# Two attention layers on one core: whole differential rows on VectorE, all key-tile remainders on GpSimd

## The chip, the core and the metric

The kernel runs on one core of one Trainium2 chip. The metric is the device time of one execution in microseconds; less is better. Five engines work at the same time, each through its own queue in order: TensorE (PE: matrix products and transposes; PEld is its weight load), VectorE (DVE), ScalarE (ACT), GpSimd (POOL), and SyncE (SP), which issues the DMAs. An instruction that waits holds up everything behind it on its engine.

## The reference

Two layers, each with one input projection that feeds three parallel branches (a state space scan, grouped-query attention, differential attention) and one output projection. 256 context tokens stand ahead of 1024 latent tokens; latent tokens read all 1280 keys, context tokens the 256 context keys. The part that matters here is the differential branch: 4 heads, two softmax maps each over the same values.

```python
def diff_attend(q, k, v, p):
    o = attention(q[:, :, 0::2], k[:, :, 0::2], v) - lam * attention(q[:, :, 1::2], k[:, :, 1::2], v)
    o = (rmsnorm(o, norm_g) * (1.0 - lam_init)).astype(v.dtype)
    return o.reshape(o.shape[0], o.shape[1], DIFF_WIDTH) * jax.nn.silu(p["dg"])
```

All is float32.

## The kernel before, in words

The program runs, for each layer, the projections with the scan (from 0 to about 571 us, and from about 1070 to 1572 us) and then the attention of both kinds, with the output projection woven into it (571 to 1070 us, and 1572 to 1995 us), and a short end. The change lies in the attention.

Attention is cut into jobs: one kind (0 grouped-query, 1 differential), one head, two or four tiles of 128 queries. A job has two sides.

The score side (`s_pair`, `s_rows`): for a tile of 128 queries PE makes the scores of 1280 keys in three PSUM banks (tile `sc`, L1259), DVE takes each from PSUM, negated and with the least value kept (L1261, into the row tile `pt`), and ACT makes the exponential of the whole row of 1280 with its sum (L1274). A differential tile of queries has two such rows. They are combined before they meet the values: row 0 plus a factor times row 1, the factor (`cc`, L1304 and L1305) being one number for each query. The combination is one DVE instruction over the columns from 0 to `cut` (L1308); what lies behind `cut` is done by two POOL instructions (L1312 scales a part of row 1, L1313 adds it to row 0). `cut` is the number of key tiles, 10, times `DC[l]`, rounded up, times 128:

```python
cut = math.ceil(jb.nk * DC[l]) * P                                   # L1307
V.scalar_tensor_tensor(dst[0][:, 0:cut], dst[1][:, 0:cut], c[:, 1:2], dst[0][:, 0:cut], ...)   # L1308
if cut < w_:
    a, b = dst[0][:, cut:w_], dst[1][:, cut:w_]
    G.tensor_scalar(b, b, c[:, 1:2], 1.0, op0=ALU.mult, op1=ALU.mult)  # L1312
    G.tensor_tensor(a, a, b, op=ALU.add)                               # L1313
```

A context job has two key tiles, so that its whole row lies within `cut` before and after.

The value side (`w_front`, `w_back`): in each step PE transposes two key tiles of two query tiles into one PSUM bank (`tp`, L1388). The product with the values runs in two fast float32 passes, so each 512 columns are split into a high part `ph` and a remainder `pl`. There are two ways. In the first, ACT rounds `tp` to `ph` (L1394) and DVE takes the remainder from PSUM (`pl<-tp,ph`, L128, the line of the helper `lo_part`). In the second, ACT copies `tp` to SBUF (`pf`, L1398), ACT or DVE in turn rounds it to `ph` (L1408 or L1410), and POOL takes the remainder (`pl<-pf,ph`, L128). `MIX` is the share of steps that go the first way while there are scores left to make; once the last scores of a layer are made, `MIXE` (0.5) holds instead. In a tenth of the last steps of layer 1 (`MIXF`) there is no split. PE then multiplies `ph` (L1430) and `pl` (L1431) with the values, three steps behind the transposes (`LAG`); `ph`, `pl` and `pf` share 8 buffers (`PWB`).

The order on each engine comes from a scheduler that goes through the whole program with its own timing of the instructions, so that another instruction in one place can move others on every engine. The tile pools add the waits.

Of the kernel before, what the change touches and what calls it, by code (L numbers as in the profile page):

```python
# [34 lines left out]
NPM = PK["convw"][0]  # L35
TOUT = 1
LEAD = 30
MIX = ((0.1, 0.1), (0.1, 0.1))
MIXE = 0.5
MIXC = ((0.5, 0.5), (0.4, 0.6))  # L40
DC = (0.8, 0.8)
MIXF = ((0.0, 0.0), (0.0, 0.1))
PWB = 8
CORD = ((0, 0), (1, 0), (1, 1), (0, 1), (1, 2), (1, 3), (0, 2), (0, 3))
# [23 lines left out]
def block_kernel(ctx: ExitStack, tc: tile.TileContext, tok, cvec, wmod, pack,  # L68
# [61 lines left out]
    def cs(c):  # L130
        return slice(c * P, (c + 1) * P)
# [303 lines left out]
    for l in range(DEPTH):  # L435
# [810 lines left out]
        with pool("att", 2) as ap, pool("attX", NXO, space=PSUM) as aX, pool("attO", NPO, space=PSUM) as aO, \  # L1246
# [49 lines left out]
            def s_pair(jb, pair):  # L1296
# [4 lines left out]
                if jb.kind == 1:  # L1301
# [4 lines left out]
                    w_ = jb.nk * P  # L1306
                    cut = math.ceil(jb.nk * DC[l]) * P  # L1307
                    V.scalar_tensor_tensor(dst[0][:, 0:cut], dst[1][:, 0:cut], c[:, 1:2], dst[0][:, 0:cut],  # L1308
# [74 lines left out]
            def w_front(jb, hf, s):  # L1383
# [3 lines left out]
                for j in range(4):  # L1387
                    TE.transpose(tp[:, j * P:(j + 1) * P], jb.pt[2 * hf + j % 2][:, cs(2 * s + j // 2)], ident)  # L1388
                mix[0] += MIX[l][jb.ph] if sdone[0] < len(squeue) else MIXE
                if mix[0] >= 1.0:  # L1390
# [250 lines left out]
```

## Time and profile before

| | us |
|---|---|
| median of 3 runs (2024.3 to 2028.09) | 2027.06 |
| the profiled execution | 2032.17 |
| its span, first to last instruction | 2030.4 |
| PE busy in the span | 1793.4 |
| DVE busy | 1369.5 |
| POOL busy | 1192.1 |
| ACT busy | 1046.7 |
| attention of layer 0 (571 to 1070) | 499 |
| attention of layer 1 (1572 to 1995) | 423 |

Busy times are sums over the span; an engine that is busy for a smaller part of it can still be what another waits for at a given place, so the waits of PE within the two attention stretches are read apart. In the rows further down a group names line, engine, operation, written and read tile, shape and count, then busy time, mean duration in ns, the idle time of the engine just before, and what ended it. In a timeline a row has its start, its duration (both us), the engine and the instruction; in brackets the idle time before it and who ended that.

### The profile page before, as it was taken

To read this page: it belongs to the slowest core of one execution; us is meant where nothing else is said; L and a number is where in the kernel's file an instruction comes from. 1 tells how busy PE (TensorE), PEld (TensorE's weight loads), DVE (VectorE), ACT (ScalarE), POOL (GpSimd) and SP (SyncE) were. 2 spreads that over 40 slices of the span, in tenths; PEclk is the share of its full clock that TensorE was granted. 3 is DMA by queue.
4 is the path that set the end of the run, shared out by engine and by line. 5 is a ranking of instruction groups with operands and counts; after the bars stand their busy time and mean duration, and the time that the engine had idled before them with its cause. 6 is when DMAs were issued, how large, how long until landed. Compare 5 with 4: busy or idle time off the path is not lost. (4 is left out here: it accounts for less than half of the span.)

```text
span 2030.4 us, 30265 instructions
## 1 busy us (share of the span) xinstructions
PE 1793.4 (88%) x9936; PEld 1457.8 (72%) x9936; DVE 1369.5 (67%) x3268; ACT 1046.7 (52%) x1971; POOL 1192.1 (59%) x1129
## 2 busy tenths in 40 slices
PE   5899999799989999988888899887899898988886
PEld 4687777687768578867675687776777677867774
DVE  3676568754566776796937586587645787887944
ACT  3554233333457766776545354333234577777651
POOL 2536355656637667777645344566566467877661
PEclk8899999899989999989799999998989999999987
DMA  9148657865787887786646158668657956566536
GB/s 285 53 129 281 206 165 204 266 221 181 226 264 237 279 283 244 230 254 196 209 166 219 46 193 268 192 196 264 210 158 213 298 158 193 163 178 204 176 117 219
DMA packets 359997, 418.57 MB, mean 206 GB/s; under 512 B 38752, under 2 KB 252832, under 8 KB 359840
## 3 DMA queue, kind: packets, MB, share of 16 engines
q1 hardware_dynamic: 359840, 416.64, 66.1%
q8 instruction: 78, 1.28, 0.3%
q14 instruction: 79, 0.65, 0.1%
HBM read 282.18 MB, written 134.38 MB: 205 GB/s over the span
## 5 line engine op out<-in xcount | busy, mean ns | idle before, releaser
L128 POOL TENSOR_TENSOR pl<-pf,ph 128x512 fp32r<-128x512 f32 x283 | 375.3, 1330 | 193.4 <-DVE ph L1410 97.7
L1261 DVE TENSOR_SCALAR_CACHE_REDUCE pt<-sc 128x512 f32<-128x512 f32 (+1 forms) x600 | 335.1, 586 | 104.8 <-PE sc L1259 90.5
L1274 ACT ACTIVATE pt<-pt,nm 128x1280 f32<-128x1280 f32 x192 | 262.2, 1366 | 109.9 <-DVE nm L1272 109.1
L976 PE MATMUL prj<-wh,u 128*128 128x512 f32 (+1 forms) x768 | 289.2, 381 | 7.3 <-ACT wh L965 5.4
L977 PE MATMUL prj<-wl,u 128*128 128x512 f32 (+1 forms) x768 | 289.3, 378 | 3.5 <-DVE wl L128 1.8
L978 PE MATMUL prj<-wh,u 128*128 128x512 f32 (+1 forms) x768 | 286.7, 375 | 0.0
L1388 PE MATMUL tp<-ident,pt 128*128 128x128 f32 x1312 | 210.3, 283 | 13.0 <-ACT pt L1274 6.2
L1398 ACT COPY pf<-tp 128x512 f32<-128x512 f32 x289 | 166.7, 581 | 81.4 <-PE tp L1388 50.1
L1431 PE MATMUL po<-pl,vt 128*128 128x256 f32 x644 | 179.7, 302 | 21.9 <-POOL pl L128 21.4
L1430 PE MATMUL po<-ph,vt 128*128 128x256 f32 x644 | 185.0, 301 | 11.7 <-ACT ot L1435 5.6
L1388 PEld LDWEIGHTS tp<-ident,pt 128*128 128x128 f32 x1312 | 161.9, 146 | 34.4 <-ACT pt L1274 8.0
L976 PEld LDWEIGHTS prj<-wh,u 128*128 128x128 f32 x768 | 149.5, 195 | 31.5 <-ACT wh L965 6.6
L977 PEld LDWEIGHTS prj<-wl,u 128*128 128x128 f32 x768 | 150.1, 196 | 29.8 <-DVE wl L128 4.5
L978 PEld LDWEIGHTS prj<-wh,u 128*128 128x128 f32 x768 | 150.0, 195 | 21.4
L1259 PE MATMUL sc<-dk,q 128*128 128x512 f32 (+1 forms) x400 | 148.9, 414 | 17.8 <-DVE pt L1261 9.6
L1431 PEld LDWEIGHTS po<-pl,vt 128*128 128x128 f32 x644 | 124.7, 194 | 38.0 <-POOL pl L128 32.0
L1430 PEld LDWEIGHTS po<-ph,vt 128*128 128x128 f32 x644 | 124.8, 194 | 32.6 <-ACT ot L1435 9.3
L1259 PE MATMUL sc<-gk,q 128*128 128x256 f32 (+1 forms) x400 | 117.4, 401 | 20.7 <-DVE pt L1261 10.1
L612 DVE SCALAR_TENSOR_TENSOR cacc<-craw,hw,cacc 128x1284 f32<-128x1284 f32 (+1 forms) x64 | 119.2, 1863 | 24.2 <-ACT cacc L609 17.3
L348 PE MATMUL ops<-y,wo 128*128 128x512 f32 (+1 forms) x304 | 118.6, 390 | 10.6 <-DMA y<-y 7.1
L587 PE MATMUL prj<-u,wTh 128*128 128x512 f32 x256 | 105.7, 413 | 14.0 <-ACT craw L603 5.6
L349 PE MATMUL ops<-y,wo 128*128 128x512 f32 (+1 forms) x304 | 114.3, 376 | 0.0
(277 smaller groups left out, 4233.1 us busy)
## 6 DMA issues: line engine op xcount, KB each, us to landing
wo<-wo SPq DMA_DIRECT2D x80, 512.0 KB, 4.5
wm<-in_wmod_dram SPq DMA_DIRECT2D x48, 512.0 KB, 5.8
dk<-dk SPq DMA_DIRECT2D x16, 1280.0 KB, 8.1
ab<-acs SPq DMA_DIRECT2D x18, 1024.0 KB, 6.8
wf<-in_wtok_dram SPq DMA_DIRECT2D x64, 256.0 KB, 3.9
wo<-wos SPq DMA_DIRECT2D x32, 512.0 KB, 3.5
y<-y SPq DMA_DIRECT2D x30, 512.0 KB, 6.1
op<-o SPq DMA_DIRECT2D x48, 256.0 KB, 4.2
```

Of the source, the lines that this page charges most:

```text
L128: eng.tensor_tensor(out_, full, hi.bitcast(F32), op=ALU.subtract)
L612: V.scalar_tensor_tensor(acc[:, a0:1284], raw[:, a0 + j:1284 + j], hw[:, i * 5 + j:i * 5 + j + 1], acc[:, a0:1284], op0=ALU.mult, op1=ALU.add)
L976: TE.matmul(ps[:, c0:], uh, wh[k][:, c0:], start=k == 0, stop=False)
L977: TE.matmul(ps[:, c0:], uh, wl[k][:, c0:], start=False, stop=False)
L978: TE.matmul(ps[:, c0:], ul, wh[k][:, c0:], start=False, stop=k == KT - 1)
L1259: TE.matmul(ps[:, 0:b - a].rearrange("p (t c) -> p t c", c=P), q[:, jb.q0 + j], kt[:, a // P:b // P], start=x == 0, stop=x == len(qq) - 1)
L1261: V.tensor_scalar(ts[r][:, a:b], ps[:, 0:b - a], -1.0, None, op0=ALU.mult, op1=ALU.min, accum_out=mts[r][:, i:i + 1])
L1274: S_.activation(e, e, AF.Exp, bias=nm, scale=-1.0, accum_out=jb.s2[:, j, mp_:mp_ + 1])
L1388: TE.transpose(tp[:, j * P:(j + 1) * P], jb.pt[2 * hf + j % 2][:, cs(2 * s + j // 2)], ident)
L1398: S_.copy(pf[:, :w_], tp[:, :w_])
L1430: TE.matmul(o, vv, a[:, c], start=k == 0, stop=False)
L1431: TE.matmul(o, vv, b[:, c], start=False, stop=k == jb.nk - 1)
```

## The change

Two numbers change. `DC` goes from 0.8 to 1.0 in both layers: `cut` becomes all 10 key tiles, so that one DVE instruction over 1280 columns takes the place of one over 1024, and the two POOL instructions over 256 go. `MIX` goes from 0.1 to 0.0: until the last scores of a layer are made, every step goes the second way.

```diff
-MIX = ((0.1, 0.1), (0.1, 0.1))
+MIX = ((0.0, 0.0), (0.0, 0.0))
 MIXE = 0.5
 MIXC = ((0.5, 0.5), (0.4, 0.6))
-DC = (0.8, 0.8)
+DC = (1.0, 1.0)
```

Counted over the program: 64 instructions of L1308 go from 1024 to 1280 columns; 64 of L1312 and 64 of L1313 go; the first way falls from 39 steps to 8; the copies `pf` rise from 289 to 320, the roundings on ACT (L1408) from 140 to 155 and on DVE (L1410) from 143 to 158, POOL's remainders from 283 to 313; one step more is without a split.

POOL, layer 1, before: the stretch that the trace has from about 1803 to 1816 us, in which two differential rows are combined.

```order
L1371 TENSOR_TENSOR oo<-oo,nrr 128x256
L128 TENSOR_TENSOR pl<-pf,ph 128x512
L1374 TENSOR_TENSOR yk<-oo,gg 128x4x64
L128 TENSOR_TENSOR pl<-pf,ph 128x512
L1312 TENSOR_SCALAR pt<-pt,cc 128x256
L1372 TENSOR_TENSOR gg<-gg,gdn_11539 128x256
L1313 TENSOR_TENSOR pt<-pt 128x256
L1312 TENSOR_SCALAR pt<-pt,cc 128x256
L128 TENSOR_TENSOR pl<-pf,ph 128x512
L1313 TENSOR_TENSOR pt<-pt 128x256
L128 TENSOR_TENSOR pl<-pf,ph 128x512 x2
```

The same place on POOL now:

```order
L1371 TENSOR_TENSOR oo<-oo,nrr 128x256
L128 TENSOR_TENSOR pl<-pf,ph 128x512
L1374 TENSOR_TENSOR yk<-oo,gg 128x4x64
L128 TENSOR_TENSOR pl<-pf,ph 128x512
L1372 TENSOR_TENSOR gg<-gg,gdn_11507 128x256
L128 TENSOR_TENSOR pl<-pf,ph 128x512 x8
```

Between the normalisation of one output tile (L1371, L1374) and the next work of that kind nothing but remainders `pl` is left in the queue.

DVE at that place, before (the first L1308 here is the one that the trace starts at 1807.74 us):

```order
L1261 TENSOR_SCALAR pt,mt<-sc 128x256
L1410 CAST ph<-pf 128x512
L1305 TENSOR_SCALAR cc<-cc,s_15810,nlam_11541 128x1
L1272 TENSOR_REDUCE nm<-mt 128x1
L1308 SCALAR_TENSOR_TENSOR pt<-pt,cc 128x1024
L1304 RECIPROCAL cc<-s_15810 128x1
L1305 TENSOR_SCALAR cc<-cc,s_15810,nlam_11541 128x1
L128 TENSOR_TENSOR ys<-yp,ys 128x4x128
L1308 SCALAR_TENSOR_TENSOR pt<-pt,cc 128x1024
L1261 TENSOR_SCALAR pt,mt<-sc 128x512 x2
```

and now, from the same row of the same head:

```order
L1304 RECIPROCAL cc<-s_15778 128x1
L1305 TENSOR_SCALAR cc<-cc,s_15778,nlam_11509 128x1
L1410 CAST ph<-pf 128x512
L1308 SCALAR_TENSOR_TENSOR pt<-pt,cc 128x1280
L128 TENSOR_TENSOR ys<-yp,ys 128x4x128
L1261 TENSOR_SCALAR pt,mt<-sc 128x256
L1261 TENSOR_SCALAR pt,mt<-sc 128x512 x2
L1272 TENSOR_REDUCE nm<-mt 128x1
```

The combination is wider, and the scheduler has put score pieces (L1261) between it and the next one.

DVE in layer 0, the first step that went the first way, before:

```order
L1308 SCALAR_TENSOR_TENSOR pt<-pt,cc 128x1024
L128 TENSOR_TENSOR pl<-tp,ph 128x512
L1261 TENSOR_SCALAR pt,mt<-sc 128x512
L1261 TENSOR_SCALAR pt,mt<-sc 128x256
L1410 CAST ph<-pf 128x512
L1261 TENSOR_SCALAR pt,mt<-sc 128x512
```

and now:

```order
L1308 SCALAR_TENSOR_TENSOR pt<-pt,cc 128x1280
L1410 CAST ph<-pf 128x512
L1261 TENSOR_SCALAR pt,mt<-sc 128x512
L1261 TENSOR_SCALAR pt,mt<-sc 128x256
L1261 TENSOR_SCALAR pt,mt<-sc 128x512
L1272 TENSOR_REDUCE nm<-mt 128x1
```

The remainder from PSUM is gone from DVE; a rounding stands in its place.

## Rows read from the trace of the kernel before

**Rows 1.** Busy us in the two attention stretches: PE, PEld, DVE, ACT, POOL.

```profile
571.00:1070.00 499.00, 449.57 (x2707) 363.82 (x2706) 358.66 (x1090) 324.29 (x594) 329.36 (x325) 0.94 0.76 237
1572.00:1995.00 423.00, 368.64 (x2219) 311.17 (x2218) 309.43 (x940) 283.08 (x483) 286.72 (x258) 0.96 0.63 190
```

**Rows 2.** Waits of PE, attention of layer 0: total us, times, longest.

```profile
PE po L1431 <- POOL pl L128: 11.6, 12, 1.9
PE sc L1259 <- DVE pt L1261: 8.3, 17, 1.3
```

**Rows 3.** Waits of PE, attention of layer 1.

```profile
PE sc L1259 <- DVE pt L1261: 11.4, 25, 1.8
PE po L1431 <- POOL pl L128: 9.8, 14, 2.2
PE sc L1259 <- DMA q<-gq: 6.3, 1, 6.3
```

**Rows 4.** Groups of POOL by form, whole span.

```profile
L128 POOL TENSOR_TENSOR pl<-pf,ph 128x512 fp32r<-128x512 f32 x283 | 375.3, 1330 | 193.4 <-DVE ph L1410 97.7 <-ACT ph L1408 55.2 <-DVE nm L1272 15.6
L1312 POOL TENSOR_SCALAR pt<-pt,cc 128x256 f32<-128x256 f32 x64 | 66.5, 1039 | 37.0 <-DVE cc L1305 26.1 <-ACT pt L1274 4.4 <-ACT ph L1408 3.9
L1313 POOL TENSOR_TENSOR pt<-pt 128x256 f32<-128x256 f32 x64 | 61.3, 958 | 2.6
```

**Rows 5.** Timeline of one place in layer 1, rows of POOL, DVE, ACT, PE.

```profile
1807.60 1.28 POOL L128 TENSOR_TENSOR pl<-pf,ph 128x512 fp32r<-128x512 f32 x1 [2.12 <-DVE ph L1410]
...
1807.74 2.23 DVE L1308 SCALAR_TENSOR_TENSOR pt<-pt,cc 128x1024 f32<-128x1024 f32 x1
...
1808.86 1.45 POOL L1312 TENSOR_SCALAR pt<-pt,cc 128x256 f32<-128x256 f32 x1
...
1809.86 0.63 ACT L1408 CAST ph<-pf 128x512 fp32r<-128x512 f32 x1
...
1810.86 1.27 DVE L1308 SCALAR_TENSOR_TENSOR pt<-pt,cc 128x1024 f32<-128x1024 f32 x1
...
1810.97 1.75 POOL L1313 TENSOR_TENSOR pt<-pt 128x256 f32<-128x256 f32 x1
...
1812.70 0.47 POOL L1312 TENSOR_SCALAR pt<-pt,cc 128x256 f32<-128x256 f32 x1
1813.14 1.26 POOL L128 TENSOR_TENSOR pl<-pf,ph 128x512 fp32r<-128x512 f32 x1
...
1814.46 0.39 PE L1431 MATMUL po<-pl,vt 128*128 128x256 f32 x1 [2.16 <-POOL pl L128]
```

**Rows 6.** Durations of two lines, ns: least, median, most; first and last start.

```profile
L616 DVE SCALAR_TENSOR_TENSOR cacc<-craw,cacc x16: 1216/1496/1498, 106.4 to 1247.3; 128x1284 f32<-128x1284 f32 x14, 128x1024 f32<-128x1024 f32 x2
L1313 POOL TENSOR_TENSOR pt<-pt x64: 715/738/1807, 600.0 to 1911.6; 128x256 f32<-128x256 f32 x64
```

**Rows 7.** Timeline of PE: first and last of twelve waits.

```profile
852.01 0.39 PE L1431 MATMUL po<-pl,vt 128*128 128x256 f32 x1 [0.38 <-POOL pl L128]
...
1896.71 0.38 PE L1431 MATMUL po<-pl,vt 128*128 128x256 f32 x1 [0.33 <-POOL pl L128]
```

**Rows 8.** A wait of DVE in the attention of layer 1.

```profile
DVE pt L1261 <- POOL pt L1313: 6.6, 6, 1.9
```

**Rows 9.** Groups of DVE by form, whole span.

```profile
L1308 DVE SCALAR_TENSOR_TENSOR pt<-pt,cc 128x1024 f32<-128x1024 f32 x64 | 96.7, 1511 | 0.6
L1410 DVE CAST ph<-pf 128x512 fp32r<-128x512 f32 x143 | 85.7, 599 | 25.7 <-ACT pf L1398 23.8 <-POOL pl L128 0.9 <-PE po L1431 0.3
L128 DVE TENSOR_TENSOR pl<-tp,ph 128x512 fp32r<-128x512 f32 x39 | 26.7, 685 | 17.5 <-ACT ph L1394 10.3 <-POOL pl L128 5.5 <-PE po L1430 1.5
```

**Rows 10.** A group of ACT by form, whole span.

```profile
L1408 ACT CAST ph<-pf 128x512 fp32r<-128x512 f32 x140 | 86.4, 617 | 7.5 <-POOL pl L128 4.5
```

**Rows 11.** Timeline of PE: first and last of fifteen waits.

```profile
597.43 1.34 PE L1259 MATMUL sc<-dk,q 128*128 128x512 f32 x3 [0.27 <-DVE pt L1261]
...
1863.70 0.50 PE L1259 MATMUL sc<-dk,q 128*128 128x512 f32 x1 [0.16 <-DVE pt L1261]
```

## The prediction

> **What bounds the kernel now.** The first view is the busy time by stretch [rows 1]. The two attention stretches are 499 and 423 us long, 922 of the span's 2030.4. PE is busy for 449.6 and 368.6 of them, so it stands idle for 49.4 + 54.4 = 103.8 us; DVE is busy for 0.72 and 0.73 of the stretches, POOL for 0.66 and 0.68, ACT for 0.65 and 0.67. The reader is to see that PE sets the time, and that work taken from POOL or DVE is worth only what it takes out of PE's idle time. So the second view is PE's waits there [rows 2, 3]. POOL's remainders `pl` hold PE for 11.6 + 9.8 = 21.4 us in 26 waits, DVE's taking of scores for 8.3 + 11.4 = 19.7 us in 42. The change touches no other wait of PE directly, and its own matmuls stay as they are but for one step, so 41.1 us, 2% of the time, is about the most that it could win.
>
> **POOL's side.** POOL loses the 64 + 64 instructions behind `cut`, 66.5 + 61.3 = 127.8 us, and gets 30 more remainders at 1.330 us, 39.9 us [rows 4]: 87.9 us less on paper. A part of the 127.8 is no work, though. At the place in layer 1 [rows 5] the scaling L1312 begins at 1808.86 and takes 1.45 us, ending 0.34 us after the combination on DVE, begun at 1807.74, is over; further down, with DVE on other work, it takes 0.47. The addition L1313 takes 0.715 at the least [rows 6]. So the work proper is 64 x (0.47 + 0.715) = 75.8 us, and the other 52 us are POOL standing beside DVE, a wait that a `pl` at that place in the queue may inherit. The relief of POOL is between 75.8 - 39.9 = 35.9 and 87.9 us.
>
> The Trainium skill (SBUF — State Buffer, section "Who interferes with whom") says that a DVE instruction with two SBUF inputs and a GpSimd instruction that reads SBUF exclude each other: whichever starts first holds the shared ports to its end and the other fully blocks. The place agrees on both sides, 1.45 against 0.47 on POOL, 2.23 against 1.27 on DVE. By the rule the lower of the two reliefs is the one that counts, and a wider combination holds POOL off for longer; that speaks against the change and is the mechanism of the third rival.
>
> On the path counts only what stood between a ready `ph` and its `pl` while PE waited. At the place [rows 5] ACT has `ph` done at 1810.49; L1313 (1.75) and L1312 (0.47) run first, `pl` begins at 1813.14, and PE has waited 2.16 us when it gets it. In 12 of the 26 waits POOL did such work between the rounding and the `pl` that PE waited for (first and last [rows 7]). Taking for each the smaller of that work and of PE's wait, they add up to 8.5 us. Bounds: 0, if the next link is late at once, and -21.4, all waits on `pl`. I take **-8.5**, the counted value.
>
> DVE too waits for L1313, before it may overwrite a row tile: 6.6 us in 6 waits of layer 1 [rows 8]. This goes. PE sees DVE only through the scores and has slack in most places: 0 to -6.6, I take **-2**, near the lower end, since 19.7 us of PE's wait stand against far more of DVE's work.
>
> **The steps that change their way.** 31 steps leave DVE's subtraction from PSUM. The chain of such a step gets longer by a rounding (about 0.6, [rows 9, 10]) and by 1.330 - 0.685 = 0.645 us for the remainder: 1.25 us x 31 = 39 us, if nothing hid it. What hides it are the three steps between a transpose and its product; without that cover PE would wait the 39. With it I charge what a `pl` of POOL costs PE today, 21.4 / 283 = 0.076 us, for 30 of them: **+2.3**. Lower bound 0 (PE's few waits on the old way would go as well). ACT gets 15 roundings of 0.617 us, 9.3 us [rows 10], and stays under 0.69 of the stretches: nothing.
>
> **DVE's side.** The combination grows by 256 columns. The nearest row is a like instruction of 1284 columns, 1.496 us in the median [rows 6], against 1.27 alone at 1024 [rows 5]: +0.23. Scaling the mean of 1.511 [rows 9] by a quarter gives +0.38. I take +0.30, 64 times: 19.2 us. The 31 subtractions leave, 21.2 us, and 15 roundings come, 9.0 us [rows 9]. DVE's net is +7.0 us in some 668. For the path: in 15 of the 42 waits of PE on scores a combination had ended on DVE less than 4 us before (first and last [rows 11]); if each grew by 0.30 that would be 4.5 us, or 0.23 of the 19.2. The same share of the net 7.0 is **+1.6**. Bounds: 0, and 19.2 if every combination came up on the path. Queued behind a combination are score pieces L1261 (as the order shows), and PE's score banks and ACT's exponentials wait for these.
>
> **The order.** The scheduler deals the instructions out anew, and SP issues the same transfers at other places. One wait for a transfer that now falls well or badly is worth up to 6.3 us [rows 3] either way. I set 0 and put it into the range.
>
> **The sum.** -8.5 - 2 + 2.3 + 1.6 = -6.6 us against the profiled execution of 2032.17: 2025.6. That execution is 5.1 us above the median of the runs shown, 2027.06; taking the same 6.6 from the median gives **2020.5 us**, 0.33% faster. This measurement can tell 0.2%, about 4 us, from no change: below 2023.0 counts as faster, above 2031.1 as slower.
>
> **The rivals.**
> 1. *POOL was the hinge, and more comes free.* `pl` also gives back the buffers that ACT's copies need and so starts the next step. If the waits on `pl` fall by two thirds (-14.3) and DVE's relief from L1313 counts in full (-6.6), with the +3.9 of the other terms: -17, 2010. For it: 52 us of POOL's time beside DVE may go as well. Against: in 14 of the 26 waits POOL did none of that work after the rounding.
> 2. *It evens out.* The 8.5 us come back as another wait, since PE's idle time is spread over many short waits, and the order moves a transfer: 2027, give or take 4. For it: DVE and POOL exchange work, and DVE is the busier of the two. Against: nothing takes PE's place as the bound.
> 3. *The lock decides, and it is slower.* The place: DVE's combinations. One that starts while POOL works on a `pl` pays for it: 2.23 in place of 1.27, +0.96 [rows 5]. On average it pays 1.511 - 1.27 = 0.24 now. POOL's queue beside differential rows now holds little but `pl`; if half of the 64 meet one, that is 31 us, 15 more than today's 15.4, and every `pl` that starts second is held for up to 1.5 us where before the scaling took that wait. Then DVE's net is 7 + 15 = 22 us, at the share of 0.23 +5; the 8.5 shrink to nothing, as 64 `pl` inherit up to 52 us of standing by, of which PE's share of 0.076 / 1.33 is 3: +5 + 3 + 2.3 - 2 = +8, 2035. It decides from the point where PE's waits on scores grow by more than those on `pl` shrink. For it: the rows on both engines. Against: POOL is idle for a third of the stretches, and the order spreads combinations out.
>
> That the change does nothing of what it says is excluded by the order: the 64 wide combinations are there, the POOL pairs are not.
>
> **How the numbers follow.** Forecast (2014 to 2023): 0.36. Rival 1 (below 2014): 0.12. Rival 2 (2023 to 2031): 0.25. Rival 3 (above 2031): 0.27. Faster is forecast and rival 1, 0.48; same 0.25; slower 0.27. A range for 8 in 10 reaches to rival 1's value and past rival 3's: 2008 to 2038. The forecast's own range is 2014 to 2023.
>
> **What would show it.** Right: POOL's busy time falls by 36 to 88 us; PE's waits on `pl` in the two stretches fall from 21.4 to about 13 + 2; those on scores stay within 3 us of 19.7; L1308 has a mean near 1.8 us. The POOL side is wrong if the waits on `pl` don't fall though the pairs are gone, or if `pl` has a mean well above 1.330 us; the DVE side is wrong if L1308 means over 2.0 us or DVE's busy time rises by more than 20 us. The whole is wrong if PE's idle time in the attention does not fall, or falls while the time outside those stretches moves.

## The result and the profile after

The changed kernel is slower: 2042.07 us in the median of 4 runs (2040.99 to 2044.84) against 2027.57 for the kernel before (2024.3 to 2033.25), a ratio of 1.0074 with a 95% interval of 1.0054 to 1.0093. The forecast was 2020.5, its range 2008 to 2038. The profiled execution took 2040.99 us, its span is 2039.2 (before 2032.17 and 2030.4).

Busy time by engine, the page's first part, of the kernel after:

```profile
PE 1792.2 (88%) x9936; PEld 1463.1 (72%) x9936; DVE 1386.2 (68%) x3252; ACT 1051.7 (52%) x1986; POOL 1139.5 (56%) x1031
```

POOL has 52.6 us less than before, DVE 16.7 more; PE has 1.2 less in the sum. So the span grew by 8.8 us without more work on PE.

Where it grew, the stretches tell if they are cut by events and not by a clock time. Here an attention stretch goes from the first score product of a layer to its last output product. First the kernel before, layer 0 and layer 1; the columns are the stretch, its length, the busy time of PE, PEld, DVE, ACT and POOL, PE's mean granted clock, the DMA share and GB/s.

```profile
570.40:1082.00 511.60, 462.13 (x2751) 371.21 (x2751) 368.81 (x1104) 331.71 (x606) 332.83 (x328) 0.94 0.76 236
1581.70:2010.10 428.40, 378.64 (x2243) 315.18 (x2246) 315.10 (x948) 287.49 (x490) 287.45 (x259) 0.96 0.63 192
```

The same two stretches of the kernel after:

```profile
569.10:1080.30 511.20, 458.39 (x2751) 370.44 (x2751) 371.99 (x1095) 334.71 (x615) 308.67 (x280) 0.94 0.76 236
1580.20:2019.20 439.00, 387.19 (x2243) 324.15 (x2246) 327.80 (x939) 291.01 (x497) 257.83 (x209) 0.93 0.61 187
```

Layer 0 is as long as it was, 511.2 against 511.6. The whole loss of this execution is in the attention of layer 1, 439.0 against 428.4. A profile is one execution only. Where the runs below have a stretch more than once in the very same order, two of its lengths lie 0.8 to 5.7 us apart; the 10.6 us here are more than that. PE has 2243 instructions there in both, and its busy time still rose, 378.6 to 387.2. The granted clock fell from 0.96 to 0.93. With full speed at 2.4 GHz and the lower level at 1.2 (granted 0.5), a mean of 0.93 is a share of 0.14 at the lower level, 61 us of 439; 0.96 is 0.08, 34 us of 428. So some 27 us more of the stretch ran at 1.2 GHz, as far as two digits of the clock can tell.

PE's waits in layer 0 after (total us, times, longest), which answer to [rows 2]:

```profile
PE sc L1259 <- DVE pt L1261: 11.5, 17, 2.3
PE po L1431 <- POOL pl L128: 10.9, 11, 2.6
```

and in layer 1, which answer to [rows 3]:

```profile
PE po L1431 <- POOL pl L128: 17.3, 17, 2.2
PE sc L1259 <- DMA q<-gq: 10.9, 2, 9.2
PE sc L1259 <- DMA q<-dq: 9.3, 3, 5.2
PE sc L1259 <- DVE pt L1261: 5.8, 12, 1.7
```

PE waits on `pl` for 28.2 us in place of 21.4, and on scores for 17.3 in place of 19.7. In layer 1 the transfers of `q` cost 20.2 us where the kernel before had 6.3 for `gq` [rows 3] and 5.3 for `dq`:

```profile
PE sc L1259 <- DMA q<-dq: 5.3, 2, 2.9
```

The groups by form, of POOL, DVE (three) and ACT, answer to [rows 4, 9, 10]:

```profile
L128 POOL TENSOR_TENSOR pl<-pf,ph 128x512 fp32r<-128x512 f32 x313 | 438.3, 1405 | 288.3 <-DVE ph L1410 119.4 <-ACT ph L1408 67.7 <-DVE nm L1272 40.7
...
L1308 DVE SCALAR_TENSOR_TENSOR pt<-pt,cc 128x1280 f32<-128x1280 f32 x64 | 112.9, 1765 | 0.9
L1410 DVE CAST ph<-pf 128x512 fp32r<-128x512 f32 x158 | 101.0, 639 | 31.4 <-ACT pf L1398 22.6 <-POOL pl L128 5.0 <-PE po L1430 2.5
L128 DVE TENSOR_TENSOR pl<-tp,ph 128x512 fp32r<-128x512 f32 x8 | 5.5, 688 | 5.6 <-ACT ph L1394 5.0 <-PE po L1430 0.6
...
L1408 ACT CAST ph<-pf 128x512 fp32r<-128x512 f32 x155 | 95.4, 616 | 4.7 <-PE po L1430 1.3 <-POOL pl L128 0.7
```

The counts are as the change has them, and the combination takes 1.765 us, as forecast. The remainder `pl` on POOL takes 1.405 in place of 1.330, 23 us over 313 of them.

How waits and clock hang together is seen at one place of layer 1, rows of PE, POOL and DVE (start, duration, and in brackets the idle time before and who ended it):

```profile
1788.77 0.39 PE L1431 MATMUL po<-pl,vt 128*128 128x256 f32 x1 [0.58 <-POOL pl L128]
...
1789.03 2.27 DVE L1308 SCALAR_TENSOR_TENSOR pt<-pt,cc 128x1280 f32<-128x1280 f32 x1
...
1790.01 0.39 PE L1431 MATMUL po<-pl,vt 128*128 128x256 f32 x1 [0.50 <-POOL pl L128]
...
1790.47 0.60 PE L1388 MATMUL tp<-ident,pt 128*128 128x128 f32 x4
...
1791.91 1.27 POOL L128 TENSOR_TENSOR pl<-pf,ph 128x512 fp32r<-128x512 f32 x1 [1.95 <-DVE ph L1410]
...
1793.23 0.58 PE L1431 MATMUL po<-pl,vt 128*128 128x256 f32 x1 [1.03 <-POOL pl L128]
...
1793.40 1.71 DVE L1308 SCALAR_TENSOR_TENSOR pt<-pt,cc 128x1280 f32<-128x1280 f32 x1
...
1794.04 1.05 PE L1388 MATMUL tp<-ident,pt 128*128 128x128 f32 x4
...
1794.12 2.11 POOL L128 TENSOR_TENSOR pl<-pf,ph 128x512 fp32r<-128x512 f32 x1 [0.37 <-ACT ph L1408]
...
1797.97 1.41 PE L1259 MATMUL sc<-dk,q 128*128 128x512 f32 x3 [2.66 <-DMA q<-dq]
```

and in the windows around it:

```profile
1782.00:1790.00 8.00, 6.92 (x48) 5.73 (x46) 6.27 (x24) 6.43 (x11) 5.03 (x4) 1.00 0.80 265
1790.00:1794.00 4.00, 2.87 (x15) 2.30 (x16) 3.23 (x8) 3.06 (x7) 1.84 (x2) 0.89 1.10 300
1794.00:1803.00 9.00, 6.34 (x26) 5.60 (x25) 4.79 (x14) 3.11 (x5) 6.42 (x7) 0.50 0.42 116
1803.00:1810.00 7.00, 7.00 (x46) 6.07 (x44) 6.53 (x22) 6.30 (x13) 4.94 (x4) 0.98 0.09 20
```

PE waits three times on `pl` within 5 us (0.58, 0.50, 1.03). From about 1793 to 1803 the granted clock is 0.50, 1.2 GHz: four transposes that took 0.60 us at 1790.47 take 1.05 at 1794.04. In that stretch PE also waits 2.66 us for a `q`. Once it is busy again the clock comes back, 0.98 from 1803 on. Waits and slower work thus stand together here, first the idle time and then the lower clock. That the waits bring the lower clock on is read from the order of the rows; no run tests it.

### The profile page after: what moved, and what is told of

Same layout as the page of the kernel before. It is cut to its first block, busy times and chain, and to the rows that moved or that the text cites. A ratio compares the mean times of both kernels' runs of the same rounds, so it can differ in the third digit from the quotient of the medians.

```text
span 2039.2 us, 30176 instructions
## 1 busy us (share of the span) xinstructions
PE 1792.2 (88%) x9936; PEld 1463.1 (72%) x9936; DVE 1386.2 (68%) x3252; ACT 1051.7 (52%) x1986; POOL 1139.5 (56%) x1031
## 5 line engine op out<-in xcount | busy, mean ns | idle before, releaser
L128 POOL TENSOR_TENSOR pl<-pf,ph 128x512 fp32r<-128x512 f32 x313 | 438.3, 1405 | 288.3 <-DVE ph L1410 119.4
L1261 DVE TENSOR_SCALAR_CACHE_REDUCE pt<-sc 128x512 f32<-128x512 f32 (+1 forms) x600 | 334.8, 588 | 102.9 <-PE sc L1259 94.4
L1398 ACT COPY pf<-tp 128x512 f32<-128x512 f32 x320 | 184.4, 581 | 69.7 <-PE tp L1388 34.9
L1431 PE MATMUL po<-pl,vt 128*128 128x256 f32 x642 | 185.1, 310 | 29.0 <-POOL pl L128 28.2
L1259 PE MATMUL sc<-dk,q 128*128 128x512 f32 (+1 forms) x400 | 150.4, 420 | 20.6 <-DVE pt L1261 10.6
L348 PE MATMUL ops<-y,wo 128*128 128x512 f32 (+1 forms) x304 | 117.9, 388 | 8.7 <-DMA y<-y 4.1
L1410 DVE CAST ph<-pf 128x512 fp32r<-128x512 f32 x158 | 101.0, 639 | 31.4 <-ACT pf L1398 22.6
L1308 DVE SCALAR_TENSOR_TENSOR pt<-pt,cc 128x1280 f32<-128x1280 f32 (+1 forms) x72 | 118.9, 1653 | 1.0
```

The costliest lines, as they stand in the source:

```text
L128: eng.tensor_tensor(out_, full, hi.bitcast(F32), op=ALU.subtract)
L1259: TE.matmul(ps[:, 0:b - a].rearrange("p (t c) -> p t c", c=P), q[:, jb.q0 + j], kt[:, a // P:b // P], start=x == 0, stop=x == len(qq) - 1)
L1261: V.tensor_scalar(ts[r][:, a:b], ps[:, 0:b - a], -1.0, None, op0=ALU.mult, op1=ALU.min, accum_out=mts[r][:, i:i + 1])
L1398: S_.copy(pf[:, :w_], tp[:, :w_])
L1431: TE.matmul(o, vv, b[:, c], start=False, stop=k == jb.nk - 1)
```

## The experiments

A ratio is the time of a kernel over that of the kernel before, run beside it on the same chip, with its 95% interval; it is worked out from all executions and can differ by about 0.001 from the quotient of the two medians. Names such as e2 or e11 are those that the expectations use for the runs. "Wide" stands for `DC` 1.0 (the combination over the whole row), "remainders" for `MIX` 0.0. The theories: **A**, the longer chain of the steps that change their way is what costs; **B**, the lock between the wide combination on DVE and `pl` on POOL; **C**, the new order that the scheduler deals out, whatever it holds; **D**, the wide combination is a real gain if the remainders stay on DVE.

### Each half alone, and the same instructions in another order

The half with the remainders alone (e1):

```diff
-MIX = ((0.1, 0.1), (0.1, 0.1))
+MIX = ((0.0, 0.0), (0.0, 0.0))
```

> Only the second half of the change: every step takes its remainder on GpSimd (MIX 0), the differential rows stay at 1024 columns on VectorE with 256 on GpSimd. The whole change cost 14.5 us (2027.6 to 2042.1). Theory A (the 31 steps whose remainder moved to GpSimd got a longer chain, and the matmuls wait for it): this kernel alone shows most of the loss, 2036 to 2044, and the PE's waits on pl rise above 26 us from 21.4. Theory B (the wide combination holds the port and stretches what GpSimd does): no loss here, 2024 to 2031. Theory C (no instruction costs more on the path; the scheduler dealt the order out anew and the loads of q and the last store of y fell badly): anywhere within 8 us of 2028, and the two halves don't add up to the whole.

Measured 2024.66 us, 0.9975 [0.9959, 0.9990], with 21.9 us of PE's waits on `pl`. The loss that A expected isn't there.

The wide half alone (e2):

```diff
-DC = (0.8, 0.8)
+DC = (1.0, 1.0)
```

> Only the first half of the change: VectorE combines all 1280 columns, the GpSimd pair is gone, one step in ten keeps its remainder on VectorE from PSUM (MIX 0.1). Theory A: 2018 to 2027, faster than before or the same, since GpSimd's queue is shorter by 64 pairs and VectorE pays 0.25 us per row. Theory B: most of the loss is here, 2036 to 2044, with a mean of the combination of 1.75 us or more and a mean of pl of about 1.40 us (1.330 before). Theory C: within 8 us of 2028, not additive with the other half.

Measured 2003.39 us, 0.9873 [0.9843, 0.9903]: each half alone is faster than before. The loss that B expected isn't there either. C had it right that the halves don't add up to the whole, but its 8 us were too few, as this kernel lies 24 us under the 2028. PE's waits on `pl` in its two attention stretches:

```profile
PE po L1431 <- POOL pl L128: 6.9, 8, 2.1
...
PE po L1431 <- POOL pl L128: 7.4, 10, 1.7
```

14.3 us, where the prediction had "about 13 + 2". The wide combination takes no longer or shorter here, and `pl` is slowed here too:

```profile
L1308 DVE SCALAR_TENSOR_TENSOR pt<-pt,cc 128x1280 f32<-128x1280 f32 x64 | 113.2, 1769 | 0.8
...
L128 POOL TENSOR_TENSOR pl<-pf,ph 128x512 fp32r<-128x512 f32 x283 | 388.6, 1378 | 309.1 <-DVE ph L1410 131.6 <-ACT ph L1408 70.2 <-DVE nm L1272 45.7
```

So B alone, with 0.048 of its 0.075 us per `pl` in the fastest kernel of all, does not make a kernel slow.

The other two runs leave the amounts of work as they are, within a few steps, and only start one of the counters elsewhere. These counters deal the steps out: the first between the two ways, the third the roundings between ACT and DVE. The scheduler then makes another order of the whole attention. In the kernel before:

```diff
-            mix = [0.0, 0.0, 0.0]
+            mix = [0.5, 0.0, 0.0]
```

> The kernel before with one thing changed that alters no amount of work: the counter that picks every tenth step starts at 0.5 in place of 0, so the same kind of steps fall five places earlier (40 in place of 39) and the scheduler deals out a new order. It measures what a new order alone is worth. Theories A and B: within 4 us of the kernel before, 2023 to 2032. Theory C: off by 8 us or more is possible, and the waits of PE for the loads of q (11.6 us in layer 1 before, 20.2 after the change) differ from before by 5 us or more.

Measured 2034.27 us, 1.0014 [0.9999, 1.0028], not clear of the kernel before, and PE's waits for `q` in layer 1 are 12.5 us against 11.6, where C expected them to move by 5 or more. In the changed kernel:

```diff
-            mix = [0.0, 0.0, 0.0]
+            mix = [0.0, 0.0, 0.5]
```

> The changed kernel with one thing changed that alters no amount of work: the counter that gives the rounding to ScalarE or VectorE in turn starts at 0.5 in place of 0, so the two swap places in the row and the order is dealt out anew. Theories A and B: within 4 us of the changed kernel, 2038 to 2046. Theory C: as far off as 2028 to 2036 is possible, since the loss is one of the order.

Measured 2033.52 us, 1.0018 [1.0003, 1.0032], 0.6% less than the changed kernel with the same work: within C's range, outside that of A and B. The next four repeat the fast halves in new orders, or go further in the same direction. Wide, `mix = [0.5, 0, 0]` (e5):

> The wide combination with every tenth remainder still on VectorE (as in the run that took 2003.4 us, 27 us under before), with the counter of the tenth steps started at 0.5, so that the same kinds of steps fall at other places and the order is new. Theory D (the wide combination is a real gain of 15 to 30 us as long as VectorE keeps some remainders, and the loss comes from taking those away): 1998 to 2012. Theory C (an order is worth 8 us or more either way by itself, and the 2003.4 was a lucky one): 2010 to 2028.

Wide, `mix = [0, 0, 0.5]` (e8):

> The same once more with the other counter shifted: ScalarE and VectorE swap places in the roundings, tenth steps as in the 2003.4 us run. Theory D: 1998 to 2012. Theory C: 2010 to 2028, and the two shifted runs differ from each other by 5 us or more.

Wide, with more remainders on DVE (`MIX` 0.2, e6):

> The wide combination with every fifth remainder on VectorE from PSUM (MIX 0.2; 0.1 before, 0.0 after). Theory D, with the chain of a GpSimd remainder as its reason: as good as MIX 0.1 or better, 1992 to 2008, since 30 more steps take the shorter chain, PE's waits on pl below 14 us. If GpSimd's relief was all of it and VectorE becomes the engine that PE waits for: 2008 to 2025, with PE's waits on the taking of scores above 20 us. Theory C: anything from 2000 to 2030.

Remainders (`DC` 0.8), `mix = [0, 0, 0.5]` (e7):

> Every remainder on GpSimd, differential rows at 1024 columns as before (2024.7 us in the first run of this), with the counter of the roundings shifted so that the order is new. Theory D, where taking the remainders from VectorE costs by itself: 2028 to 2040, the 2024.7 having been a good order. If it costs only together with the wide combination: 2020 to 2030. Theory C: within 10 us of 2028.

Measured 2020.66 (0.9968 [0.9951, 0.9984]), 2021.01 (0.9965 [0.9951, 0.9979]), 2018.11 (0.9947 [0.9931, 0.9964]) and 2018.24 (0.9951 [0.9928, 0.9974]). The wide half is faster each time, but its first order was worth some 19 us more than the two new ones (0.9873 against 0.9968 and 0.9965): outside D's range, inside C's, though these two lie closer together than C had it. With `MIX` 0.2 PE's waits on `pl` fall to 12.8 us, as D expected, those on scores are 21.4, and the kernel is not faster than its fellows with 0.1. And e7, where D expected 2028 or more if the remainders cost by themselves, came out faster than the kernel before. Effects of the halves and of an order are of like size, so nothing can be read from one order of each.

### Layer by layer

Wide in both layers, the remainders moved in one layer only. First in layer 1:

```diff
+MIX = ((0.1, 0.1), (0.0, 0.0))
+DC = (1.0, 1.0)
```

> DC 1.0 in both layers, MIX 0.1 in layer 0 and 0.0 in layer 1. Up to the first scores of layer 1 the order on every engine is that of the run with DC 1.0 and MIX 0.1 (567.9 + 501.0 + 497.1 = 1566 us there), and every theory expects these 1566 us again, give or take 3. Order theory: the attention of layer 1, newly dealt, falls anywhere between the 415.5 and 439.0 us seen so far, profiled 2001 to 2025. Theory that the two halves spoil each other (wide combinations with all remainders on POOL): 431 to 439 us in the attention of layer 1, PE's waits on pl there near 17 us as in the changed kernel, 2017 to 2025. The result tells them apart only if the stretch comes out below 425 us, which speaks against the second.

then in layer 0:

```diff
+MIX = ((0.0, 0.0), (0.1, 0.1))
+DC = (1.0, 1.0)
```

> DC 1.0 in both layers, MIX 0.0 in layer 0 and 0.1 in layer 1. The order is that of the changed kernel through layer 0 and the projections of layer 1 (569.1 + 511.2 + 499.9 = 1580 us there) and then that of the run with DC 1.0 and MIX 0.1 (415.5 us for the attention of layer 1, 20 for the end). Order theory: the two pieces add up, 2016 us profiled, give or take 5. If what comes before (the state of the queues at the start) matters as much as the order itself: the attention of layer 1 misses 415.5 by over 5 us. Theory that the halves spoil each other: the same 2016, since the second half is then alone in layer 1.

Measured 2008.51 (0.9910 [0.9884, 0.9936]) and 2017.32 (0.9942 [0.9924, 0.9959]). The attention stretches of wide alone (layer 0, layer 1):

```profile
567.90:1068.90 501.00, 458.84 (x2751) 369.28 (x2751) 376.52 (x1104) 330.70 (x607) 288.76 (x265) 0.95 0.78 241
1566.00:1981.60 415.60, 373.25 (x2243) 315.61 (x2246) 321.25 (x948) 287.48 (x490) 234.07 (x195) 0.97 0.65 197
```

of the first of the two kernels:

```profile
566.00:1062.80 496.80, 452.23 (x2751) 363.46 (x2751) 377.88 (x1104) 330.43 (x607) 288.37 (x265) 0.96 0.78 243
1559.80:1982.60 422.80, 379.70 (x2243) 319.89 (x2246) 319.80 (x940) 290.55 (x497) 254.89 (x209) 0.95 0.63 194
```

and of the second:

```profile
568.30:1083.20 514.90, 459.95 (x2751) 371.58 (x2751) 371.77 (x1095) 335.08 (x615) 308.33 (x280) 0.94 0.76 234
1581.00:1995.80 414.80, 372.32 (x2243) 315.44 (x2246) 321.13 (x947) 287.13 (x490) 234.18 (x195) 0.96 0.64 197
```

An order keeps its length from kernel to kernel within a few us: the second has the order of the kernel after in layer 0 (514.9 against 511.2) and that of wide alone in layer 1 (414.8 against 415.6), and the pieces add up to the 2016 expected, within the 5 us allowed. The first has that of wide alone in layer 0 (496.8 against 501.0); it reached the scores of layer 1 at 1559.8, 6 us before the 1566 that was expected within 3, so that one execution scatters by more than was allowed there. In layer 1 the first has both halves at work in a third order, and takes 422.8 us there, below the 425 that were to count against a cost of both halves, where the kernel after takes 439.0. So both halves together don't need 439 us.

### The lock, and six pairs of orders

The combination in two pieces, so that a `pl` can start between them:

```diff
+for a_, b_ in ((0, cut // 2), (cut // 2, cut)):
+    V.scalar_tensor_tensor(dst[0][:, a_:b_], dst[1][:, a_:b_], c[:, 1:2], dst[0][:, a_:b_], ...)
```

> The changed kernel with each combination as two DVE instructions of 640 columns, so that a pl that waits for DVE's ports can start between the halves. It adds 64 instructions to DVE. Lock theory: pl's mean falls from 1.405 to 1.35 us or less, PE's waits on pl from 28.2 to below 20 us, the time to 2025 to 2033. Order theory: pl's mean may fall likewise, but the time goes where the new deal puts it, 2015 to 2045, and does not follow pl's mean.

Measured 2052.62 us, 1.0111 [1.0078, 1.0145]. Its `pl`, its combinations, and PE's waits on `pl` and on scores in layer 0 and in layer 1:

```profile
L128 POOL TENSOR_TENSOR pl<-pf,ph 128x512 fp32r<-128x512 f32 x313 | 421.1, 1351 | 314.2 <-DVE ph L1411 135.3 <-ACT ph L1409 70.0 <-DVE nm L1272 38.9
...
L1309 DVE SCALAR_TENSOR_TENSOR pt<-pt,cc 128x640 f32<-128x640 f32 x128 | 146.7, 1186 | 0.8
```

```profile
PE sc L1259 <- DVE pt L1261: 14.5, 21, 2.2
...
PE po L1432 <- POOL pl L128: 4.5, 8, 1.1
...
PE sc L1259 <- DVE pt L1261: 11.8, 23, 2.1
PE po L1432 <- POOL pl L128: 11.6, 12, 2.2
```

The mean of `pl` fell to 1.351 and PE's waits on it from 28.2 to 16.1 us, as B said, yet the kernel got slower, beyond what either theory expected. The two pieces cost DVE 146.7 us where the whole rows cost 112.9, and PE waits 26.3 us on scores in place of 17.3. The run thus adds a price of its own and doesn't weigh the lock by itself; it does show that the time does not follow `pl`'s mean.

To part C from a cost of both halves together, wide alone and both halves were each run with the same six pairs of starting values of the first and the third counter. Equal values don't make equal orders on the two sides, so the pairs are in fact two sets of six. Nor are the six all different everywhere: in layer 0, where the roundings go to ACT and DVE in turn, starts of 0 and 0.3 give the same order of instructions on DVE, ACT and POOL in the traces, and so do 0.5 and 0.7. Each set has six orders in layer 1 and four in layer 0. Both halves, third counter at 0.3 (e11; the text on record says of this counter that it deals the last part; it deals the roundings throughout):

> The changed kernel with the same instructions in another order (the counter that deals the steps' ways in the last part starts at 0.3). Order theory: the time moves by several us and by another amount than the 8.5 that the first such re-deal gained; anything from 2015 to 2045. Theory that the two halves spoil each other, whatever the order: 2030 to 2045, as in the two deals seen (2042, 2033.5). Lock theory: pl keeps a mean of 1.36 to 1.41 us and the time stays above 2030.

Measured 2025.12 us: below what the lock and a cost in every order had expected. What is left to ask is whether there is such a cost in the mean. Wide alone, 0.3 (e13); wide alone, 0.7 (e14); both, 0.7 (e15); both, 0.5 and 0.5 (e16); wide alone, 0.5 and 0.5 (e17); both, 0.5 and 0 (e18):

> DC 1.0, MIX 0.1, in a fourth order (the counter that deals the roundings out between ACT and DVE starts at 0.3). To be set beside both halves in the run e11 (2025.1 us), which starts that counter at the same value. Theory that order alone decides: 2003 to 2042, on either side of e11 with equal chance. Theory that both halves together have a cost of their own: 2003 to 2021, below e11.

> DC 1.0, MIX 0.1, in a fifth order (the counter starts at 0.7), the partner of e15. Order alone: 2003 to 2042, either side of e15. A cost of both halves together: 2003 to 2021, 10 to 20 us below e15.

> Both halves (the changed kernel) in a fourth order (the counter starts at 0.7), the partner of e14. Order alone: 2003 to 2042, either side of e14, and as likely as not below 2020. A cost of both halves together: 2025 to 2042, 10 to 20 us above e14.

> Both halves in a fifth order (this counter at 0.5, and the one that deals the steps between the two ways at 0.5 too), the partner of e17. Order alone: 2003 to 2042, either side of e17. A cost of both halves together: 2025 to 2042, 10 to 20 us above e17.

> DC 1.0, MIX 0.1, in a sixth order (both counters start at 0.5), the partner of e16. Order alone: 2003 to 2042, either side of e16. A cost of both halves together: 2003 to 2021, 10 to 20 us below e16.

> Both halves in a sixth order (the counter that deals the steps between the two ways starts at 0.5), the partner of e5 (2020.7 us). Order alone: 2003 to 2042, either side of e5. A cost of both halves together: 2025 to 2042, 5 to 20 us above e5.

| first and third counter | wide alone: ratio, attention of layers 0 and 1 (us) | both halves: ratio, attention of layers 0 and 1 | difference |
|---|---|---|---|
| 0, 0 | 0.9873, 501.0, 415.6 | 1.0074 (the kernel after), 511.2, 439.0 | 0.0201 |
| 0, 0.5 | 0.9965, 511.2, 421.2 | 1.0018, 516.3, 431.2 | 0.0053 |
| 0.5, 0 | 0.9968, 506.0, 422.1 | 0.9991 [0.9969, 1.0013], 513.8, 425.1 | 0.0023 |
| 0, 0.3 | 0.9904 [0.9879, 0.9929], 498.1, 418.3 | 0.9992 [0.9977, 1.0007], 509.2, 423.9 | 0.0088 |
| 0, 0.7 | 0.9983 [0.9967, 0.9999], 506.5, 425.1 | 1.0036 [1.0021, 1.0051], 514.0, 428.6 | 0.0053 |
| 0.5, 0.5 | 0.9964 [0.9946, 0.9982], 509.5, 424.1 | 1.0044 [1.0025, 1.0064], 515.4, 432.0 | 0.0080 |
| mean | 0.9943, 505.4, 421.1 | 1.0026, 513.3, 429.9 | 0.0083 |

Three things follow. The same instructions, within a few steps, lie 1.1% (22 us) apart from the best order to the worst for wide alone, 0.8% (17 us) for both halves: C is right that an order can be worth as much as either edit. Both halves are slower than wide alone in all six pairs and in both layers of each, by 0.0083 in the mean (from the spread of the six, plus or minus 0.0065), 17 us. The first pair is the one that raised the question; the other five give 0.0059, plus or minus 0.0032, 12 us. Each pair run after that question came out on the side that a cost of both halves called for, though e14, at 2022.37 us, lies 1.4 us above its range. So there is also such a cost of the remainders on POOL beside wide combinations, and C alone falls. And the kernel after is the worst of its six orders, 0.0048 or 10 us above their mean.

Where the 17 us are, the six profiles show in the mean: PE's idle time in the two stretches goes from 90.2 to 100.9 us, its waits on `pl` from 14.6 to 21.9, those on scores from 17.0 to 21.3; its busy time goes from 836.2 to 842.3 us, with 112 us in place of 92 at 1.2 GHz. DVE's busy time there is the same (699 us in both), POOL's goes from 521 to 562. So it is not DVE's load. Nor is it POOL's load or the waits on `pl` by themselves: with `DC` at 0.8 and the remainders moved (e1, e7) POOL is busy for 661 us of the stretches and PE waits 21.9 and 29.4 us on `pl`, and both kernels are faster than before. Nor is it the lock's price for a `pl`: its mean is 1.392 us over the six of wide alone and 1.386 over the six of both. Where the cost shows is thus known; why it needs both halves is not.

The best of the new orders of both halves, for the attention of layer 1 and PE's waits there:

```profile
1578.90:2002.80 423.90, 379.53 (x2243) 316.52 (x2246) 326.86 (x939) 290.98 (x497) 256.62 (x209) 0.96 0.64 194
```

```profile
PE sc L1259 <- DVE pt L1261: 12.4, 25, 1.5
PE po L1431 <- POOL pl L128: 11.7, 16, 2.3
PE sc L1259 <- DMA q<-gq: 9.4, 2, 9.1
...
PE sc L1259 <- DMA q<-dq: 2.9, 2, 2.1
```

Against the kernel after, with the same instructions: 15.1 us shorter, 7.7 of them in PE's busy time at a clock of 0.96 in place of 0.93, the rest in idle time, with 5.6 us less on `pl`, 7.9 less on `q` and 6.6 more on scores.

## Why the prediction was wrong

**The order: "I set 0 and put it into the range".** This step failed. The measured time lies 21.6 us above the forecast. Some 10 of them are the order's, as the kernel after is the worst of its six; the other 12 lie between the forecast, 0.997 of the kernel before, and the mean of the six, 1.0026: the next term was some 17 too small, and the wide half gave some 5 more than forecast. The step allowed 6.3 us either way, the price of one wait for a transfer. Twelve runs put the scatter from best to worst at 17 to 22 us. What it left out is that an order moves many waits at once, and the clock goes with them: some 27 us more at 1.2 GHz in layer 1, and PE's busy time up by 8.5 us in the same number of instructions. Where the kernel before stands among its own orders is not known, as only two of them were run (1 and 1.0014).

**The steps that change their way: +2.3.** This was mis-sized. With what they give back on DVE's side (0.23 of 12.2, 2.8 us) the moved steps were to cost about nothing; six pairs measure 17 us (plus or minus 13), or 12 (plus or minus 6.5) without the first pair, beside wide combinations. I charged each moved step what an average `pl` of POOL costs PE, 0.076 us, although the same paragraph had their chain 1.25 us longer and 39 us without cover; 17 / 31 is 0.54 us for a step. The six pairs show the cost as 7.3 us more of waits on `pl`, 4.3 on scores and 6.1 of busy time. The longer chain alone doesn't explain it, since the same steps with the same chain cost nothing beside narrow combinations, 0.9975 and 0.9951.

**POOL's side: -8.5 and -2.** For the wide half alone this was right, and rather small. PE's waits on `pl` are then 14.3 us in its first order and 14.6 in the mean of six, from 21.4; the whole half was forecast at -8.5 - 2 + 4.4 (a share of 0.23 of 19.2) = -6.1 us and measures 0.0057, 11.6 us (plus or minus 9, from the spread of the six). With the remainders moved as well the waits on `pl` are back at 21.9 in the mean, and 28.2 in the kernel after: what the one edit takes off these waits, the other puts back. So by its own sign, "if the waits on `pl` don't fall though the pairs are gone, or if `pl` has a mean well above 1.330 us", the POOL side was wrong for the two edits together (28.2 and 1.405 us).

**DVE's side: +1.6.** The durations were right in the main (the combinations +16.2 us where 19.2 was forecast; the remainders -21.2; the roundings +15.3 where 9.0 was, as their mean rose from 599 to 639 ns), and so was that PE's wait on scores stays within 3 us of 19.7. DVE's busy time rose by 16.7 us, below the 20 that were to count against it.

**The lock (rival 3).** It gave a time near the measured one, 2035, for a reason that the runs don't bear out; that is luck. The lock is there: the `pl` at 1794.12 that starts beside a combination takes 2.11 us, the one at 1791.91 that ends before it 1.27. This agrees with the rule of the Trainium skill (SBUF — State Buffer, section "Who interferes with whom") by which the two block each other. Rival 3 had DVE pay 15 us more for it. But, counted in the traces, only 33 of the 64 wide combinations start while POOL is at work, in place of 50 of the narrow ones, as the POOL pairs are gone; over what a row takes clear of POOL, 1.55 us, they pay 14 us, about the 15 of before. On POOL the price did rise: 32 of the 313 `pl` start within a combination (2.21 us in the mean, the others 1.31), in place of 8 of 283. Yet in the fastest kernel these means are nearly the same, 1.769 us for the combination and 1.378 for `pl` against 1.765 and 1.405, and score waits did not grow, which was its point of decision.

**The test of the whole** was named rightly: "PE's idle time in the attention does not fall". By the stretches above (length less PE's busy time) it went from 99.2 to 104.6 us.

**Open.** Why the remainders on POOL cost 12 to 17 us beside wide combinations is not shown. With `DC` at 0.8 the remainders cost nothing, in two orders 0.9975 and 0.9951 against 1 and 1.0014 for the kernel before. Two orders are few, so it isn't settled either that the wide combinations turn the sign of this edit. Nor is which of the waits in a cluster comes first.

The version to take is the wide half alone: faster in all six runs, 2003.39 us in the order dealt without any shift, 1.3% below the kernel before.

## What to carry to other kernels

Where a scheduler deals the order, one timing of a change is one draw: time the same instructions in several orders, before and after, before you believe a difference of 1%. Two edits that are each harmless or better alone can cost time together, so time them apart and together. And don't carry a price per step from today's average to steps that move: the same 31 steps cost nothing beside narrow combinations and 12 to 17 us beside wide ones.

## What the runs showed of the hardware

In layer 1 of the kernel after PE is busy for 8.5 us more with as many instructions, at a granted clock of 0.93 in place of 0.96. The stretch at 1.2 GHz from 1793 to 1803 came after short waits, 0.50 to 1.03 us each, while PE was still busy for 2.87 of 4 us, and the transposes in it took 1.05 us in place of 0.60. Between the means of the two sets of six profiles, 20.8 us more at 1.2 GHz went with 6.1 us more of busy time, 0.3 us for each.

Cutting a combination in two made its sum dearer, 146.7 us against 112.9. Counted in the trace, 73 of the 128 pieces started while POOL was at work and took 1.42 us in the mean, the others 0.88: each piece can meet the lock anew. Two free pieces, 1.76 us, also take longer than a free row, 1.55.
